# Two thirds of a gate product done as seven half products per unit

## The chip, the cores and the metric

The kernel runs on one core of a Trainium2 chip. TensorE (PE) does the matrix products, VectorE (DVE), ScalarE (ACT) and GpSimd (POOL) the element-wise work, and SyncE (SP) issues most DMAs. The time is the device time of one execution in microseconds, and a kernel is judged by the median of its runs. The kernel before takes 2010.5 us (three runs, 2009.51 to 2011.86).

## The reference

One layer for 1024 prompt frames and 32 sample frames, 1056 tokens of width 1024 in all. After attention, the recurrence and their mixing, the layer ends so:

```python
x = x + rms_norm(mix @ w_out, g_post_mix)
a, u = split(rms_norm(x, g_pre_ffn) @ w_up)             # 1024 -> 2 * 2816
ffn = (gelu(causal_conv3(a)) * u) @ w_down              # 2816 -> 1024
x = x + rms_norm(ffn, g_post_ffn)                       # called x2 below
y = x + (pe @ w_ple) * sigmoid(x @ w_ple_gate)          # 1024 -> 1024, the gate
```

All of it is float32. The change concerns `x @ w_ple_gate` and what it is added into.

## The kernel before

**Precision.** Every large product is made of three. Each operand is split into a high part, rounded to the type that PE multiplies in, and a low part, the rest; then high times high, high times low and low times high are summed in PSUM. `product` (L195 to L202) does that: for each of the k tiles of 128 rows three matmuls, L200, L201 and L202. A split costs ACT a copy (the high part) and DVE a subtraction (the low part): `split` at L223/L224 for activations, `load_next` at L181/L184 for weights.

**Layout and tiling.** Activations are held with the features on the 128 partitions and the tokens along the free axis. From w_down on, the tokens are worked in three thirds of 352 (`G3`, counted g = 0, 1, 2).

**w_up.** The stage before w_down multiplies by Winograd's form of Strassen's scheme: a 2 by 2 block product is done with seven half products instead of eight. The loop is `up_unit`. For every unit DVE and ACT make seven weight operands (`unit_parts`, L1444/L1445), POOL makes their four sums of 128x512 (L1451, L1452, L1453, L1458), and DVE joins the seven results out of PSUM (L1678 to L1694). The operands come out of a ring of eight buffers (tag `wb`).

**w_down.** `for g in range(3)`: for each half q of the output columns, 11 slabs of weights pass by, each used for four banks of PSUM. `d_out` copies the results to `acc` and sums their squares. When a third is through, `x2_start` and `x2_rows` make the norm's row factors, and `x2_part` makes one tile of 128x352 of x2 each time it is called: a scaled multiply (L1818), an addition of x1 (L1819), which a DMA brings in, and the split into `xh`, `xl` (L223, L224). For the first two thirds this is spread over the next third's w_down; for the last third it is spread over the gate stage.

**The gate stage.** Four weight tiles at a time are held (`ws`), and for each the thirds pass by: 24 blocks of 24 matmuls, each one bank of PSUM. `y_out` takes a block out: a tanh on ACT (L1861), then two DVE instructions (L1862 and L1863), the second with a factor 0.5 that makes a sigmoid of the tanh; `pl`, the product `pe @ w_ple`, is read back from memory by a DMA. `y_done`, one block later, turns the tile with three PE transposes (L1875), copies it on ACT (L1888, L1889), and every second tile goes to memory.

**Order.** The program order in the file is the priority; a scheduler fixes each engine's order when the kernel is built, and on the chip each engine goes through its own list in that order, waiting on semaphores. So an instruction that waits holds up everything behind it on its engine. SP's list of DMAs is one such list. A tile pool gives buffers by tag, and a new tile of a tag waits until an earlier one is released; tag `t` has six buffers, which the squares, the x1 tiles and the y tiles share.

Of the kernel before, what the change touches and what calls it, by code (L numbers as in the profile page):

```python
# [10 lines left out]
F32 = mybir.dt.float32  # L11
# [6 lines left out]
P = 128  # L18
D = 1024
KT = 8  # L20
# [39 lines left out]
def layer_kernel(  # L60
# [17 lines left out]
    def nm(s):  # L78
        n_names[0] += 1
        return f"{s}_{n_names[0]}"  # L80
# [56 lines left out]
    def rows_cols(src, r0, c, n, kt):  # L137
        return src[0, r0:r0 + kt * P, c:c + n].rearrange("(k p) c -> p k c", p=P), kt, n
# [81 lines left out]
    def split(hi, lo, src, scale=None):  # L220

        if scale is None:
            S.copy(hi, src)  # L223
            V.tensor_tensor(lo, src, hi.bitcast(F32), op=ALU.subtract)  # L224
# [10 lines left out]
    def mm_bank():  # L235
        return bank(pp, "mm", 3)
# [936 lines left out]
    with right("mp") as mp:  # L1173
# [238 lines left out]
    def ple_product(g, beside):  # L1412
        xs = pT.pop(g)
        for c in range(8):
            if c % 4 == 0:
                t = oz.tile([P, 4, H], F32, tag="x4", name=nm("ple"), bufs=3)
            b = block(ple_w[c // 4], slice((c % 4) * P, (c % 4 + 1) * P),
                      [xs[:, 0, k, :] for k in range(2)], [xs[:, 1, k, :] for k in range(2)],
                      ((0, 0), (1, 1)), H)
            S.copy(t[:, c % 4, :], b[:, :H])  # L1420
# [43 lines left out]
    def part_tile(i=0):  # L1464
        return wp.tile([P, 2, 4, P], F32R, tag="wb", name=nm("wt"), bufs=8)
# [266 lines left out]
    for u in range(NF):  # L1732
        if u == 1:
            Up = page(lq, 2, [P, 2, T], "Up")
        if u == NF - 1:
            limit[0] = len(plan)
            load_raw()
            load_raw()
        up_unit(u)
# [4 lines left out]
    def page_at(s, shape, name):  # L1744
        return page(lq if s[0] == "l" else rp, s[1:], shape, name)
# [31 lines left out]
    xh, xl = [None] * 3, [None] * 3  # L1777

    def d_out(g, c, b):
        S.copy(acc[g][c].bitcast(F32), b[:, :M3])  # L1780
# [8 lines left out]
    def x2_start(g):  # L1789
        rss[g] = norm_sums(ep, sqd[g], T96, 1.0 / D)  # L1790

    todo = []
    x2_r = {}

    def x2_rows(g):
        rb = ep.tile([P, M3], F32, tag="rb", name=nm("rb"), bufs=2)
        norm_rows(rss[g], T96, rb[:])
        if g == 0:
            x2_r[0] = page_at("l5", [P, 6, M3], "x2r")
            xh[0], xl[0] = third("r4", x2_r[0], 0, "xh"), third("l2", x2_r[0], 1, "xl")  # L1800
        elif g == 1:
            x2_r[1] = page_at("l3", [P, 6, M3], "x2r")
            xh[1] = third(chunk_at[0][0], x2_r[1], 0, "xh")
            xl[1] = third(chunk_at[0][1], x2_r[1], 1, "xl")
        else:
            xh[2] = third(chunk_at[1][0], x2_r[0], 2, "xh")
            xl[2] = third(chunk_at[1][1], x2_r[1], 2, "xl")
        todo.extend((g, k, rb) for k in range(KT))

    def x2_part(count=1, upto=-1):  # L1810

        while todo and (count > 0 or todo[0][0] <= upto):
            count -= 1
            g, k, rb = todo.pop(0)
            x1 = ep.tile([P, M3], F32, tag="t", name=nm("x1"), bufs=6)
            dma(x1[:], x1_d[:, k, M3 * g:M3 * g + M3])
            ak = acc[g][k].bitcast(F32)
            V.scalar_tensor_tensor(ak, ak, g_pffn[:, k:k + 1], rb[:], op0=ALU.mult, op1=ALU.mult)  # L1818
            V.tensor_tensor(ak, ak, x1[:], op=ALU.add)  # L1819
# [26 lines left out]
    for s, dst in ((0, o_pconv), (1, o_sconv)):  # L1846
        b = tr_bank()
# [3 lines left out]
        dma(dst[0, 0].rearrange("j (f p) -> (j f) p", p=P), t[:])  # L1851


    def y_out(g, c, b):
        y = ep.tile([P, M3], F32, tag="t", name=nm("y"), bufs=6)
        pl = ep.tile([P, M3], F32, tag="pl", name=nm("pl"), bufs=3)
        dma(pl[:], ple_d[:, c, M3 * g:M3 * g + M3])
        a = acc[g][c].bitcast(F32)
        cols = [slice(0, M3)] if (g, c) != (2, 7) else [slice(c_, c_ + m_) for c_, m_ in T96]
        for z_ in cols:  # L1860
            S.activation(y[:, z_], b[:, z_], AF.Tanh, scale=0.5)  # L1861
            V.scalar_tensor_tensor(y[:, z_], y[:, z_], 1.0, pl[:, z_], op0=ALU.add, op1=ALU.mult)  # L1862
            V.scalar_tensor_tensor(y[:, z_], y[:, z_], 0.5, a[:, z_], op0=ALU.mult, op1=ALU.add)  # L1863
        return y

    late, yrs = [], {}

    def y_done(g, c, y):

        if c % 2 == 0:  # L1870
            yrs[g] = ep.tile([P, 3, 256], F32, tag="yr", name=nm("yr"), bufs=4)
        yr = yrs[g]
        t = tr_bank()
        for i, (c_, m_) in enumerate(T96):
            E.transpose(t[:m_, i * P:(i + 1) * P], y[:, c_:c_ + m_], ident[:])  # L1875
        col = (c % 2) * P
        o = M3 * g
        fc = slice((c - 1) * P, (c + 1) * P)
# [9 lines left out]
        S.copy(yr[:, 0:2, col:col + P], t[:, :2 * P].rearrange("p (a b) -> p a b", b=P))  # L1888
        S.copy(yr[:96, 2, col:col + P], t[:96, 2 * P:3 * P])  # L1889
        if c % 2:  # L1890
            dma(y_prompt[0, o:o + 2 * P, fc].rearrange("(a p) c -> p a c", p=P), yr[:, 0:2, :])
            dma(y_prompt[0, o + 2 * P:o + 2 * P + m_, fc], yr[:m_, 2, :])
            if m_ < 96:
                dma(y_sample[0, :, fc], yr[m_:96, 2, :])

    for q in range(2):
        ws = [next_w(0) for _ in range(4)]
        for g in range(3):
            x2_part(0, g)
            for c in range(4):  # L1900
                if q == 0 and g == 0 and c == 1:
                    x2_start(2)
# [4 lines left out]
                late.append((g, 4 * q + c, y_out(g, 4 * q + c, b)))  # L1907
                if len(late) > 1:
                    y_done(*late.pop(0))
    for l in late:  # L1910
        y_done(*l)


# [30 lines left out]
```

## Time and profile before

| | |
|---|---|
| median of 3 runs | 2010.5 us |
| the profiled execution: time | 2014.52 us |
| the profiled execution: span, first to last instruction | 2012.8 us |
| granted TensorE clock, mean | 0.996 |
| PE busy in the span | 1985.5 us |
| DVE, ACT, POOL busy in the span | 1433.6, 965.6, 226.2 us |

The profile gives, for one execution, each engine's busy time, groups of instructions by line, single instructions in order of time, and waits. A group's row is: line, engine, operation, output from inputs, shape, count | busy us, mean ns of one | idle time before. A row of the instructions in order of time is: start in us, duration, engine, line, operation, names, count, and in brackets the idle time before it and what ended it. Matmuls overlap one another, so that the distance from one start to the next, and not the duration, tells how fast PE goes; the same holds, by less, for DVE and ACT.

### The profile page before, as it was taken

What the parts mean: (1) busy time and instruction counts of PE and PEld (TensorE: products, weight loads), DVE (VectorE), ACT (ScalarE), POOL (GpSimd) and SP (SyncE); (2) the same over time, 40 slices, a digit from 0 to 9 for tenths busy, and PEclk for the clock granted to TensorE, in tenths of its full rate; (3) what the DMA queues carried; (4) which work ended last, traced back from release to release, by engine and by line L of the source; (5) the groups of instructions that cost most, each with busy time, mean ns of one, the idle gap of its engine ahead of it and who ended that gap; (6) DMA issues with size and microseconds to landing.
All of it is one profiled execution on the core that took longest, in us unless ns stands there. A gap on an engine that the chain in (4) does not pass through costs nothing.

```text
span 2012.8 us, 37342 instructions
## 1 busy us (share of the span) xinstructions
PE 1985.5 (99%) x14282; PEld 1955.1 (97%) x14282; DVE 1433.6 (71%) x3193; ACT 965.6 (48%) x2184; POOL 226.2 (11%) x318
## 2 busy tenths in 40 slices
PE   7999999999999999999999999999999999999998
PEld 6999999999999999999999999999999999999998
DVE  5788888688888888554455778788887884655552
ACT  5655566556666666542124763333333344444432
POOL 2010100000000000002001123332333310000000
PEclk8999999999999999999999999999999999999999
DMA  8322321411111111377558582222222246655542
GB/s 263 96 94 68 115 64 53 144 54 57 37 54 37 54 53 56 118 229 230 165 167 291 164 296 64 85 75 85 68 92 65 88 137 202 214 190 172 167 129 82
DMA packets 250807, 245.31 MB, mean 122 GB/s; under 512 B 13365, under 2 KB 218696, under 8 KB 250629
## 3 DMA queue, kind: packets, MB, share of 16 engines
q1 hardware_dynamic: 242085, 214.92, 34.2%
q0 software_dynamic: 8464, 27.94, 3.9%
q8 instruction: 112, 1.84, 0.4%
q14 instruction: 66, 0.54, 0.1%
q10 hardware_dynamic: 80, 0.07, 0.0%
HBM read 177.56 MB, written 65.32 MB: 121 GB/s over the span
## 4 chain that ended last, share of the span: by engine, by line
PE 85%; DVE 5%; issue 2%; DMA 1%; ACT 1%; POOL 1%; SPq 0%; POOLq 0%; ACTq 0%; DVEq 0%
PE mm L200 13%; PE mm L201 13%; PE mm L202 13%; PE st L1667 7%; PE st L1665 7%; PE st L1666 7%; PE G L839 2%; PE Y L836 2%; PE G L838 2%; PE G L836 2%; PE Y L839 2%; PE Y L838 2%; PE tr L469 1%; PE X L836 1%; PE so L1030 1%
## 5 line engine op out<-in xcount | busy, mean ns | idle before, releaser
L1665 PE MATMUL st<-op,wt 128*128 128x264 f32 x1232 | 349.1, 284 | 3.7 <-ACT ple L1420 2.3
L1667 PE MATMUL st<-op,wt 128*128 128x264 f32 x1232 | 350.2, 284 | 0.0
L1666 PE MATMUL st<-op,wt 128*128 128x264 f32 x1232 | 348.4, 283 | 0.0
L184 DVE TENSOR_TENSOR wl<-wr,wh 128x1024 fp32r<-128x1024 f32 x132 | 161.6, 1225 | 129.3 <-ACT wh L181 115.5
L1665 PEld LDWEIGHTS st<-op,wt 128*128 128x128 f32 x1232 | 231.8, 188 | 4.8 <-ACT ple L1420 2.5
L1666 PEld LDWEIGHTS st<-op,wt 128*128 128x128 f32 x1232 | 232.1, 188 | 0.0
L1667 PEld LDWEIGHTS st<-op,wt 128*128 128x128 f32 x1232 | 231.5, 188 | 0.0
L181 ACT CAST wh<-wr 128x1024 fp32r<-128x1024 f32 x116 | 121.8, 1050 | 200.8 <-PE mm L201 146.5
L200 PE MATMUL mm<-ac,wh 128*128 128x352 f32 x528 | 170.7, 323 | 0.9 <-DVE Sp L1694 0.9
L201 PE MATMUL mm<-ac,wh 128*128 128x352 f32 x528 | 169.1, 320 | 0.0
L202 PE MATMUL mm<-ac,wl 128*128 128x352 f32 x528 | 169.1, 320 | 0.0
L1444 ACT CAST wt<-wu 128x512 fp32r<-128x512 f32 x126 | 77.7, 619 | 188.4 <-POOL ab L1651 93.7
L200 PE MATMUL mm<-La,wh 128*128 128x384 f32 (+1 forms) x504 | 166.2, 330 | 0.3 <-ACT kt L340 0.3
L201 PE MATMUL mm<-Lb,wh 128*128 128x384 f32 (+1 forms) x504 | 162.2, 322 | 0.0
L202 PE MATMUL mm<-La,wl 128*128 128x384 f32 (+1 forms) x504 | 162.2, 322 | 0.0
L200 PE MATMUL mm<-Ra,wh 128*128 128x264 f32 x512 | 145.5, 284 | 0.0
L201 PE MATMUL mm<-Rb,wh 128*128 128x264 f32 x512 | 145.0, 283 | 0.0
L202 PE MATMUL mm<-Ra,wl 128*128 128x264 f32 x512 | 145.0, 283 | 0.0
L1445 DVE TENSOR_TENSOR wt<-wu,wt 128x512 fp32r<-128x512 f32 x126 | 101.2, 806 | 39.7 <-ACT wt L1444 39.7
L453 ACT ACTIVATE sc<-sc,st 128x257 f32<-128x257 f32 (+1 forms) x144 | 69.6, 485 | 74.8 <-DVE st L448 73.6
L200 PEld LDWEIGHTS mm<-ac,wh 128*128 128x128 f32 x528 | 99.0, 188 | 1.2 <-DVE Sp L1694 1.2
L201 PEld LDWEIGHTS mm<-ac,wh 128*128 128x128 f32 x528 | 99.2, 188 | 0.0
(478 smaller groups left out, 5732.6 us busy)
## 6 DMA issues: line engine op xcount, KB each, us to landing
wr<-in_w_down_dram SPq DMA_DIRECT2D x66, 512.0 KB
wu<-in_w_up_dram SPq DMA_DIRECT2D x42, 512.0 KB
wu<-in_w_in_dram SPq DMA_DIRECT2D x32, 512.0 KB
wr<-in_w_in_dram SPq DMA_DIRECT2D x26, 512.0 KB
ac<-act_d SPq DMA_DIRECT2D x66, 176.0 KB
act_d<-Up SPq DMA_DIRECT2D x21, 528.0 KB
wr<-in_w_out_dram SPq DMA_DIRECT2D x16, 512.0 KB
pw_d<-pw POOLq DMA_DIRECT2D x11, 512.0 KB, 5.1
```

The costliest lines, as they stand in the source:

```text
L181: S.copy(hi[:], raw[:])
L184: V.tensor_tensor(lo[:], raw[:], hi[:].bitcast(F32), op=ALU.subtract)
L200: E.matmul(ps, wh, a, start=first and n == 0, stop=False)
L201: E.matmul(ps, wh, b, start=False, stop=False)
L202: E.matmul(ps, wl, a, start=False, stop=last and n == len(ks) - 1)
L836: E.matmul(o, wh, x[0][k], start=first and k == 0, stop=False, skip_group_check=True)
L838: E.matmul(o, wh, x[1][k], start=False, stop=False, skip_group_check=True)
L839: E.matmul(o, wl, x[0][k], start=False, stop=k == 3, skip_group_check=True)
L1445: V.tensor_tensor(t[:, 1], src, t[:, 0].bitcast(F32), op=ALU.subtract)
L1665: E.matmul(o, wh, xh, start=first and k == 0, stop=False, skip_group_check=True)
L1666: E.matmul(o, wh, xl, start=False, stop=False, skip_group_check=True)
L1667: E.matmul(o, wl, xh, start=False, stop=k == 3, skip_group_check=True)
```

## The change

The gate product of the first two thirds (704 tokens) is done as in w_up, by seven half products. The weight is cut into four units of 256 output columns; each unit is a 2 by 2 block of 512 by 128, and the two thirds of x2, each cut in two halves of 512 features, are the other 2 by 2 block. A half product is 12 matmuls (four k tiles of three) of 352 columns. The last third keeps blocks of 24.

- The activation operands for the seven products (`gate_ops`, 14 steps) are made while the last third of w_down runs (`op_steps`). For this x2 of the second third is made earlier, two tiles at a time in the first half of that third, and x2 of the first two thirds is no longer split itself.
- The weights of the units come as quarters of 128 rows by 4 by 128, 16 in all through five buffers (`quarter_load`), and `gate_parts` makes the seven operands of each unit from them, three products ahead in program order (`gate_prepare(n + 3)`). The four sums of a unit are made by DVE for the first unit and by POOL for the other three. For the last third the same weight is loaded again in eight tiles.
- `gate_unit` joins the seven results: one ACT copy and five DVE instructions per unit, from PSUM. Three of a unit's four outputs then go through `y_out` in place, their last addition on POOL; the fourth, and the last third's outputs, are added on DVE.
- `x2_start(2)`, `x2_rows(2)` and the eight `x2_part` calls of the last third stand after the half products n = 1, 3 and 5 to 12.
- `y_done` is called two half products later, not one block later. The buffers for its output go from four to three.
- The factor 0.5 moves to the exit of `pe @ w_ple` far earlier (`S.mul` for `S.copy`, L1420), so that the last step of `y_out` is a plain addition.

The diff, cut to its core:

```diff
-            S.copy(t[:, c % 4, :], b[:, :H])
+            S.mul(t[:, c % 4, :], b[:, :H], 0.5)
...
-            split(xh[g][k], xl[g][k], ak)
+            if g == 2:
+                split(last_x(0, k), last_x(1, k), ak)
...
+    def gate_parts():
+        def parts(src):
+            t = part_tile()
+            S.copy(t[:, 0], src)
+            V.tensor_tensor(t[:, 1], src, t[:, 0].bitcast(F32), op=ALU.subtract)
+            gate_w.append(t)
+        for u in range(4):
+            n = 4 * u
+            a11, a21, a22, a12 = (quarters[(n + i) % 5] for i in range(4))
+            s1 = wp.tile([P, 4, P], F32, tag="wb", name=nm("sa"), bufs=8)[:]
+            adder = V if u == 0 else G
+            parts(a11)
+            adder.tensor_tensor(s1, a21, a22, op=ALU.add)
+            adder.tensor_tensor(a21, a11, a21, op=ALU.add)
+            adder.tensor_tensor(a11, a11, s1, op=ALU.add)
+            yield
+            parts(a11)
+            yield
+            parts(a12)
+            adder.tensor_tensor(a12, a12, a11, op=ALU.add)
+            quarter_load(n + 5)
+            yield
...
-                if g == 1 and (q or k > 8) or g == 2 and q:
+                if g == 1 and (q or k > 8):
                     x2_part()
+                if g == 2 and q == 0 and 8 < k < 18:
+                    x2_part(2)
+                if g == 2:
+                    op_steps({18: 1, 20: 1}.get(k, 0) if q == 0 else
+                             {0: 1, 2: 2, 4: 1, 6: 1, 8: 1, 12: 1, 14: 2, 16: 1, 18: 1, 20: 1}.get(k, 0))
+                    if q and k == 18:
+                        gate_first()
+                    if q and k == 20:
+                        gate_prepare(3)
...
-            V.scalar_tensor_tensor(y[:, z_], y[:, z_], 0.5, a[:, z_], op0=ALU.mult, op1=ALU.add)
+            adder.tensor_tensor(y[:, z_], y[:, z_], a[:, z_], op=ALU.add)
...
+    def gate_unit(u):
+        X, Y, Z = (mm_bank() for _ in range(3))
+        x, y, zz = (t[:, :M3] for t in (X, Y, Z))
+        s1c, U2, nU3 = (um[:, i] for i in range(3))
+        c = 2 * u
+        for i, (t, first) in enumerate(((x, True), (y, True), (x, False), (y, False), (zz, True),
+                                        (y, False), (zz, False))):
+            n = 7 * u + i
+            gate_prepare(n + 3)
+            if n == 25:
+                limit[0] = len(plan)
+                load_next()
+            w = gate_w[n]
+            for k in range(4):
+                h, r = k // 2, k % 2
+                a, b = gate_rows(i, 0, h)[:, r, :], gate_rows(i, 1, h)[:, r, :]
+                E.matmul(t, w[:, 0, k, :], a, start=first and k == 0, stop=False,
+                         skip_group_check=True)
+                E.matmul(t, w[:, 0, k, :], b, start=False, stop=False, skip_group_check=True)
+                E.matmul(t, w[:, 1, k, :], a, start=False, stop=k == 3, skip_group_check=True)
+            if n == 1:
+                x2_start(2)
+            if n == 3:
+                x2_rows(2)
+            if n > 4:
+                x2_part()
...
+            if i == 0:
+                S.copy(s1c, x)
+            elif i == 1:
+                V.tensor_tensor(U2, s1c, y, op=ALU.subtract)
+            elif i == 2:
+                late.append((n, 0, c, y_out(0, c, x, r)))
+            elif i == 3:
+                V.tensor_tensor(nU3, y, s1c, op=ALU.subtract)
+            elif i == 4:
+                V.tensor_tensor(r, nU3, zz, op=ALU.subtract)
+                late.append((n, 1, c + 1, y_out(1, c + 1, r, r)))
+            elif i == 5:
+                V.tensor_tensor(r, y, s1c, op=ALU.subtract)
+                late.append((n, 0, c + 1, y_out(0, c + 1, r, r)))
+            else:
+                V.tensor_tensor(r, U2, zz, op=ALU.add)
+                late.append((n, 1, c, y_out(1, c, r, r)))
+            while late and late[0][0] + 2 <= n:
+                y_done(*late.pop(0)[1:])
...
-    for q in range(2):
-        ws = [next_w(0) for _ in range(4)]
-        for g in range(3):
-            x2_part(0, g)
-            for c in range(4):
-                if q == 0 and g == 0 and c == 1:
-                    x2_start(2)
-                if q == 0 and g == 0 and c == 3:
-                    x2_rows(2)
-                b = block(ws[c], ALL, xh[g], xl[g], KS, M3)
+    for u in range(4):
+        gate_unit(u)
+    xh, xl = ([last_x(part, k) for k in range(KT)] for part in range(2))
+    for c in range(8):
+        w = next_w(2)
+        b = block(w, ALL, xh, xl, KS, M3)
+        late.append((0, 2, c, y_out(2, c, b)))
+        while len(late) > 1:
+            y_done(*late.pop(0)[1:])
```

More of the change, by code (lines that the diff above doesn't have):

```diff
@@ L1735, in layer_kernel @@
         if u == NF - 1:
-            limit[0] = len(plan)
+            limit[0] = len(plan) - 8
             load_raw()
@@ L1776, in layer_kernel, with slots, gate_rows @@
     sqd = [None] * 3
-    xh, xl = [None] * 3, [None] * 3
+    slot_pages, slot_tiles = ("l5", "l3", "r4", "l2", "l4", "r3", "l6", "r5", "l7", "r6", "r0", "r7"), {}
+    def slots(n, m):
+        p = n // 6
+        if p not in slot_tiles:
+            slot_tiles[p] = page_at(slot_pages[p], [P, 6, M3], "gx")
+        return slot_tiles[p][:, n - 6 * p:n - 6 * p + m, :]
+    gate_at = {4: 0, 1: 8, 5: 16, 0: 24, 2: 32, 3: 40, 6: 48}
+    def gate_rows(j, part, h):
+        return slots(gate_at[j] + 4 * part + 2 * h, 2)
     def d_out(g, c, b):
@@ L1792, in layer_kernel @@
     todo = []
-    x2_r = {}
     def x2_rows(g):
@@ L1797, in x2_rows @@
         norm_rows(rss[g], T96, rb[:])
[L1798 to L1807, printed above, removed]
         todo.extend((g, k, rb) for k in range(KT))
@@ L1819, in x2_part, with last_x, gate_ops, rows @@
             V.tensor_tensor(ak, ak, x1[:], op=ALU.add)
-            split(xh[g][k], xl[g][k], ak)
+            if g == 2:
+                split(last_x(0, k), last_x(1, k), ak)
+    def last_x(part, k):
+        return slots(56 + 8 * part + k, 1)[:, 0, :]
+    um = ep.tile([P, 3, M3], F32, name="um")
+    def gate_ops():
+        def rows(g, k):
+            return acc[g][k], acc[g][k + 1]
+        def parts(j, h, src):
+            hi, lo = gate_rows(j, 0, h), gate_rows(j, 1, h)
+            if isinstance(src, tuple):
+                for i in range(2):
+                    split(hi[:, i, :], lo[:, i, :], src[i].bitcast(F32))
+            else:
+                split(hi, lo, src)
+        def sums(a, b, op):
+            for i in range(2):
+                p, q = (x[i].bitcast(F32) if isinstance(x, tuple) else x[:, i, :] for x in (a, b))
+                V.tensor_tensor(t[:, i, :], p, q, op=op)
+        t = um[:, 0:2, :]
+        b11, b21 = ([rows(0, o + 2 * h) for h in range(2)] for o in (0, 4))
+        b12, b22 = ([rows(1, o + 2 * h) for h in range(2)] for o in (0, 4))
+        for h in range(2):
+            sums(b11[h], b12[h], ALU.subtract)
+            parts(4, h, t)
+            yield
+            sums(b22[h], t, ALU.add)
+            parts(1, h, t)
+            yield
+            sums(b21[h], t, ALU.subtract)
+            parts(5, h, t)
+            yield
+        for j, b in ((0, b11), (2, b21)):
+            for h in range(2):
+                parts(j, h, b[h])
+                yield
+        for h in range(2):
+            sums(b12[h], b22[h], ALU.subtract)
+            parts(3, h, t)
+            yield
+        for h in range(2):
+            parts(6, h, b22[h])
+            yield
@@ new lines, in layer_kernel, with quarter_load, gate_first @@
+    quarters, gate_w = [], []
+    def quarter_load(n):
+        if n >= 16:
+            return
+        u, j = divmod(n, 4)
+        c, k0 = ((2 * u, 0), (2 * u + 1, 0), (2 * u + 1, 4), (2 * u, 4))[j]
+        dma(quarters[n % 5], rows_cols(w_ple_gate, k0 * P, c * P, P, 4)[0])
+    def gate_first():
+        for _ in range(2):
+            t = wp.tile([P, 2, 4, P], F32, tag="wr", name=nm("wr"), bufs=2)
+            quarters.extend(t[:, i] for i in range(2))
+        quarters.append(ep.tile([P, 4, P], F32, name="wr5")[:])
+        for n in range(5):
+            quarter_load(n)
@@ new lines, in gate_parts @@
+    def gate_parts():
[13 more added lines that the diff above has]
+            adder.tensor_tensor(a11, a11, s1, op=ALU.add)
+            yield
+            parts(a11)
+            yield
+            parts(a12)
+            adder.tensor_tensor(a12, a12, a11, op=ALU.add)
+            quarter_load(n + 5)
+            yield
+            parts(a21)
+            quarter_load(n + 6)
+            yield
+            parts(s1)
+            yield
+            parts(a22)
+            quarter_load(n + 7)
+            yield
+            parts(a12)
+            quarter_load(n + 8)
+            yield
@@ L1822, in layer_kernel, with gate_prepare, op_steps @@
+    gate_gen, op_gen = gate_parts(), gate_ops()
+    def gate_prepare(n):
+        while len(gate_w) < min(n + 1, 28):
+            next(gate_gen)
+    def op_steps(n):
+        for _ in range(n):
+            next(op_gen)
     for g in range(3):
@@ L1851, in layer_kernel, with y_out @@
         dma(dst[0, 0].rearrange("j (f p) -> (j f) p", p=P), t[:])
-    def y_out(g, c, b):
-        y = ep.tile([P, M3], F32, tag="t", name=nm("y"), bufs=6)
+    def y_out(g, c, b, y=None):
+        adder = V if y is None else G
+        if y is None:
+            y = ep.tile([P, M3], F32, tag="t", name=nm("y"), bufs=6)
         pl = ep.tile([P, M3], F32, tag="pl", name=nm("pl"), bufs=3)
@@ L1868, in y_done @@
     def y_done(g, c, y):
-        if c % 2 == 0:
-            yrs[g] = ep.tile([P, 3, 256], F32, tag="yr", name=nm("yr"), bufs=4)
-        yr = yrs[g]
+        second = (g, c // 2) in yrs
+        if not second:
+            yrs[g, c // 2] = ep.tile([P, 3, 256], F32, tag="yr", name=nm("yr"), bufs=3)
+        yr = yrs[g, c // 2]
         t = tr_bank()
@@ L1877, in y_done @@
         o = M3 * g
-        fc = slice((c - 1) * P, (c + 1) * P)
+        fc = slice((c // 2) * 256, (c // 2 + 1) * 256)
         m_ = min(96, 1024 - o - 2 * P)
@@ L1889, in y_done @@
         S.copy(yr[:96, 2, col:col + P], t[:96, 2 * P:3 * P])
-        if c % 2:
+        if second:
             dma(y_prompt[0, o:o + 2 * P, fc].rearrange("(a p) c -> p a c", p=P), yr[:, 0:2, :])
@@ L1894, in y_done @@
                 dma(y_sample[0, :, fc], yr[m_:96, 2, :])
-    for q in range(2):
-        ws = [next_w(0) for _ in range(4)]
-        for g in range(3):
-            x2_part(0, g)
-            for c in range(4):
-                if q == 0 and g == 0 and c == 1:
-                    x2_start(2)
-                if q == 0 and g == 0 and c == 3:
-                    x2_rows(2)
-                b = block(ws[c], ALL, xh[g], xl[g], KS, M3)
-                x2_part()
-                late.append((g, 4 * q + c, y_out(g, 4 * q + c, b)))
-                if len(late) > 1:
-                    y_done(*late.pop(0))
+    def gate_unit(u):
[23 more added lines that the diff above has]
+            if n > 4:
+                x2_part()
+            r = None
+            if i in (2, 4, 5, 6):
+                r = ep.tile([P, M3], F32, tag="t", name=nm("y"), bufs=6)[:]
+            if i == 0:
[12 more added lines that the diff above has]
+                late.append((n, 0, c + 1, y_out(0, c + 1, r, r)))
+            else:
+                V.tensor_tensor(r, U2, zz, op=ALU.add)
+                late.append((n, 1, c, y_out(1, c, r, r)))
+            while late and late[0][0] + 2 <= n:
+                y_done(*late.pop(0)[1:])
@@ L1910, in layer_kernel @@
+    for u in range(4):
[7 more added lines that the diff above has]
+            y_done(*late.pop(0)[1:])
     for l in late:
-        y_done(*l)
+        y_done(*l[1:])
 _INS = ['x_prompt', 'x_sample', 'cache_win_k', 'cache_win_v', 'state_hgrn', 'cache_ffn_conv',
```

## The prediction

> **What bounds the kernel now.** I read the page first: busy shares, then the chain that ended last.
>
> ```profile
> span 2012.8 us, 37342 instructions
> PE 1985.5 (99%) x14282; PEld 1955.1 (97%) x14282; DVE 1433.6 (71%) x3193; ACT 965.6 (48%) x2184; POOL 226.2 (11%) x318
> ...
> PE 85%; DVE 5%; issue 2%; DMA 1%; ACT 1%; POOL 1%; SPq 0%; POOLq 0%; ACTq 0%; DVEq 0%
> ```
>
> PE bounds the whole, so fewer matmuls can pay. What they pay is decided in the stage that changes, so next the busy times by stretch: a piece of w_down, its last third, and the gate stage.
>
> ```profile
> 1660.00:1740.00 80.00, 80.00 (x506) 80.00 (x505) 41.18 (x45) 36.41 (x49) 0.00 (x0) 1.00 0.64 212
> 1906.00:2006.00 100.00, 99.86 (x649) 99.16 (x648) 43.55 (x89) 29.41 (x85) 0.00 (x0) 1.00 0.39 111
> ...
> 1827.54:1909.34 81.80, 81.80 (x522) 81.73 (x520) 43.03 (x66) 32.08 (x48) 0.00 (x0) 1.00 0.48 158
> ```
>
> Columns: stretch, its length, busy PE, PE loading, DVE, ACT, POOL with counts, clock, DMA share, GB/s. PE has no gap in the gate stage, DVE and ACT are less than half busy, POOL does nothing. In w_down a matmul of 352 columns takes 80.00/506 = 0.158 us of PE. The gate stage has 576 of them (91.0 us); its other small PE instructions, 72 transposes and 12 for the norm, share the rest of the 100 us, about 0.125 us each, so the three transposes of an output tile cost 0.375.
>
> **What the change removes.** Two thirds: 16 blocks x 24 = 384 matmuls become 28 x 12 = 336. 48 x 0.158 = 7.6 us of PE, 0.38%; it cannot gain more, since nothing else is taken from PE. The same transposes stay.
>
> **What it adds, step by step.** A half product takes PE 12 x 0.158 = 1.9 us. Beside each, DVE now must do more than beside a block of 3.8 us. Its prices are the distances between starts, in the list of DVE's instructions in the gate stage (first row: the norm's first small operation, second: its last):
>
> ```profile
> 1909.89 0.22 DVE L1260 TENSOR_SCALAR nv<-tr 128x2 f32<-128x2 f32 x2 [2.01 <-PE tr L1257]
> ...
> 1912.78 0.16 DVE L217 SCALAR_TENSOR_TENSOR nr<-rst,nr 128x3 f32<-128x3 f32 x1
> ...
> 1919.07 0.53 DVE L1863 SCALAR_TENSOR_TENSOR y<-y,acc 128x352 f32<-128x352 f32 x1
> 1919.52 1.07 DVE L1818 SCALAR_TENSOR_TENSOR acc<-acc,gvec,rb 128x352 f32<-128x352 f32 x2
> 1920.51 0.52 DVE L1819 TENSOR_TENSOR acc<-acc,x 128x352 f32<-128x352 f32 x1
> 1920.94 1.08 DVE L1818 SCALAR_TENSOR_TENSOR acc<-acc,gvec,rb 128x352 f32<-128x352 f32 x2
> 1921.93 0.53 DVE L224 TENSOR_TENSOR xl<-acc,xh 128x352 fp32r<-128x352 f32 x1
> 1922.37 1.08 DVE L1818 SCALAR_TENSOR_TENSOR acc<-acc,gvec,rb 128x352 f32<-128x352 f32 x2
> ```
>
> An output's step (either of y_out's two on DVE) costs 0.45 us; a tile of x2 costs 0.495 (half of 0.99) + 0.43 + 0.44 = 1.37; the norm holds DVE for 3.0 (1909.89 to 1912.94). For the weight operands, the joins and POOL's sums the w_up stage has the rows; DVE first, then POOL in the same stretch:
>
> ```profile
> 1307.47 1.65 DVE L1622 SCALAR_TENSOR_TENSOR a<-ab,cvec,a 128x1058 f32<-128x1058 f32 x1 [1.34 <-ACT a L1621]
> 1309.15 2.23 DVE L1623 SCALAR_TENSOR_TENSOR a<-ab,cvec,a 128x1058 f32<-128x1058 f32 x1
> ...
> 1316.07 0.68 DVE L1445 TENSOR_TENSOR wt<-wu,wt 128x512 fp32r<-128x512 f32 x1
> 1316.66 0.70 DVE L1683 TENSOR_TENSOR Sp<-st,Sp 128x528 f32<-128x528 f32 x1
> 1317.28 1.46 DVE L1445 TENSOR_TENSOR wt<-wu,wt 128x512 fp32r<-128x512 f32 x1
> ```
>
> ```profile
> 1306.70 1.29 POOL L1451 TENSOR_TENSOR sa<-wu 128x512 f32<-128x512 f32 x1 [8.86 <-PE st L1667]
> 1308.07 2.19 POOL L1452 TENSOR_TENSOR wu<-wu,wu 128x512 f32<-128x512 f32 x1
> 1310.34 2.19 POOL L1453 TENSOR_TENSOR wu<-wu,sa 128x512 f32<-128x512 f32 x1
> ...
> 1316.89 1.30 POOL L1458 TENSOR_TENSOR wu<-wu 128x512 f32<-128x512 f32 x1 [4.33 <-DVE wt L1445]
> ```
>
> ```profile
> L1678 DVE TENSOR_TENSOR Sp<-Sp,st 128x528 f32<-128x528 f32 x21 | 14.5, 692 | 0.0
> ...
> L1685 DVE TENSOR_TENSOR us<-Sp,st 128x264 f32<-128x264 f32 x1 | 0.4, 423 | 0.0
> ```
>
> ```profile
> L1623 DVE SCALAR_TENSOR_TENSOR a<-ab,cvec,a 128x1058 f32<-128x1058 f32 x1 | 1.3, 1317 | 0.0
> ```
>
> A weight operand costs DVE 0.6 us (1316.07 to 1316.66). A join of 352 columns lies between 0.423 (264) and 0.692 (528): 0.51 long, some 0.08 of it overlapped as in the rows above, 0.43. POOL's sum of 512 takes 1.29 alone, so one of 352 some 0.89. And the two engines hold each other up: L1445, 0.68 alone, took 1.46 beside L1458, 0.77 lost (L1683, which reads PSUM, lost nothing); L1623, 1.32 in the last unit, where POOL does nothing, took 2.23 beside L1452, 0.91 lost; L1622 lost 0.33. POOL's own sums went from 1.29 to 2.19. I charge DVE 0.77 for each sum of 512, the row of the very instruction that the change uses, and 0.53 (0.77 x 352/512) for each of 352.
>
> On that the Trainium skill, "SBUF — State Buffer", section "Who interferes with whom", is stricter: a DVE instruction with two SBUF inputs and a GpSimd one that reads SBUF exclude each other, and the loser blocks for the whole instruction. The trace agrees: L1452 ended at 1310.26, 1.11 us after L1623 began, and 1.11 + 1.32 is 2.43 against 2.23 measured. What the rule would give here is the third rival below.
>
> **The sum.** The heavy stretch is products 2 to 13: the norm, all eight x2 tiles, and POOL's sums for units 1 and 2.
> - PE: 144 matmuls x 0.158 = 22.75, six outputs' transposes 2.25, the norm's twelve small ones 1.5: 26.5 us.
> - DVE: norm 3.0; 12 operands x 0.6 = 7.2; 9 joins x 0.43 = 3.9; 10 output steps x 0.45 = 4.5; 8 x2 tiles x 1.37 = 10.9: 29.5 us.
> - POOL's hold on DVE: 8 sums of 512 x 0.77 = 6.2, 6 of 352 x 0.53 = 3.2: 9.4 us. (Nothing at the low end; all its time, 8 x 1.29 + 6 x 0.89 = 15.6, at the high end.)
>
> DVE needs 38.9 us where PE needs 26.5: 12.4 too many. Two things soften it. In products 0 and 1 DVE has 3.8 - 2.1 = 1.7 us free to make operands ahead. And each join has one product's time before PE needs its bank: 1.9 - 0.43 = 1.5. Once DVE is later than that, PE stops at the join, because joins stand in the same list behind x2 tiles and operands. PE stalls 12.4 - 1.7 - 1.5 = 9.2 us (low end 29.5 - 26.5 - 3.2, nothing; high end 15.4).
> - Products 14 to 27: DVE fits (7 operands, 5 joins, 5 output steps per unit, 8.6 of 14.8 us, and POOL's 4.7), except the burst 18 to 20, where four sums and three outputs meet: 9.1 against 6.5, less 1.5: 1.1 us (0 to 3).
> - POOL orders its three sums for the next unit ahead of an output's addition; at 2.19 each an output can be 6 us late, where its transposes come two products, 3.8 us, later and all matmuls stand behind them. Up to 2.8 us in each of three units; I take 1.0 in all (0 to 8), as sums start as soon as a buffer comes free (what ended L1451's idle time was PE).
> - Start: product 0 needs the first operand, whose quarter is asked for at k = 18, two slabs (7.6 us) before w_down ends. A DMA of activations took 4.64 (row below), the split 0.6 + 0.6, and DVE then makes three sums at 0.6: 7.6 us for the second operand, due 1.9 after the end. I take 1.0 (0 to 3) for waiting behind the last squares.
>
> ```profile
> 1635.47 4.64 DMA ac<-act_d
> ```
>
> Hidden, at nothing: the 14 operand steps in w_down's last third add some 17 us to DVE's 43.0 of 81.8, and ACT's to its 32.1; without that room they would cost PE 17. ACT in a unit: seven copies, one join, four tanh, four exits, 9.2 us of 14.8, from these rows:
>
> ```profile
> L1861 ACT ACTIVATE y<-mm 128x352 f32<-128x352 f32 x23 | 10.7, 464 | 51.8 <-PE mm L202 51.8
> ...
> L1888 ACT COPY yr<-tr 128x256 f32<-128x256 f32 x23 | 8.5, 370 | 0.4 <-PE tr L1875 0.3
> ...
> L1889 ACT COPY yr<-tr 96x128 f32<-96x128 f32 x23 | 6.2, 271 | 0.0
> ```
>
> ```profile
> L1444 ACT CAST wt<-wu 128x512 fp32r<-128x512 f32 x122 | 75.3, 618 | 185.4 <-POOL ab L1651 93.7 <-PE st L1667 67.7 <-DVE wt L1445 23.9
> ```
>
> The 0.5 at L1420: a copy of 264 columns takes 389 ns, one scaled by a vector (L1279) 487; at worst 0.1 us on ACT under six matmuls, and nothing (at most 0.3) on PE. The weight is read twice, 4 MB more in 90 us where 111 GB/s flow: nothing. SP issues 16 quarter loads among those of `pl` and x1; the one behind POOL's fourth sum waits for it and holds the next `pl`, a loss inside the 0 to 8 above.
>
> ```profile
> L1420 ACT COPY ple<-mm 128x264 f32<-128x264 f32 x32 | 11.8, 389 | 6.4 <-PE mm L202 5.3 <-DMA ple_d<-ple 1.0
> ...
> L1279 ACT ACTIVATE z<-mm,gph 128x264 f32<-128x264 f32 x9 | 4.4, 487 | 4.4 <-PE mm L202 4.4
> ```
>
> Total: -7.6 + 9.2 + 1.1 + 1.0 + 1.0 = +4.7 us. On the profiled execution, span 2012.8 and time 2014.52, that is 2017.5 and 2019.2. That execution stands 4.0 above the median of the runs; on the median, 2010.5 + 4.7 = 2015.2. The ends of all terms: -7.6 and -7.6 + 15.4 + 3 + 8 + 3 = +21.8.
>
> **The rivals.**
> A, faster: POOL hardly delays DVE, because its sums fall where DVE waits or reads PSUM, as L1683 beside L1458. Then the heavy stretch costs nothing (29.5 - 26.5 is under 3.2) and with the three small terms at half, 1.6, the time is 2010.5 - 6.0 = 2004.5. For it: L1622 lost only 0.33. Against it: DVE has no idle time there. It decides where the 14 sums cost DVE less than 0.2 us each.
> B, no change: x2's later steps slide. In the profile before, additions of x1 came one per block (they wait for tag `t`), and only the first multiplies ran ahead. If the additions and splits, 0.87 x 8 = 7.0 us, reach products 14 to 27, where DVE has room, the stall is 2.2 and not 9.2: 2008.2. Against it: their place in the order is 5 to 12, and a waiting addition blocks DVE.
> C, much slower: the full exclusion. POOL's 15.6 us all fall on DVE, the stall is 15.4, the others as I took them: 2010.5 - 7.6 + 15.4 + 3.1 = 2021.4, and up to 2027 if an output's addition also stops PE twice.
>
> **How the numbers follow.** My forecast (its own range 2011 to 2019) has 0.36, A 0.27, B 0.19, C 0.18. The last row of chances counts from 0.2%, 4.0 us, about what a measurement of this kernel can tell: A is faster; B is within, and 0.06 of the forecast's lower part; the rest of it and C slower: 0.27, 0.25, 0.48. The range leaves out half of A's gain below 2004 and C above 2023.
>
> **What would show it.** In the profile after: 48 matmuls fewer at 0.158; DVE near 9 tenths busy in the first two units, PE gaps there put down to DVE's joins (U2, nU3, r); L1445's counterpart and the x2 steps above 0.7 beside POOL's sums; units 0 and 1 some 4 and 5 us longer than 14.8, units 2 and 3 near it. Wrong, if the units run at 14.8 each or if the waits are on ACT, quarters or transposes.

## The result, and the profile after

The changed kernel takes 2018.9 us (median of 6 runs, 2017.64 to 2019.92), the kernel before 2011.75 beside it. The ratio is 1.0036, 95% interval 1.0023 to 1.0049: slower by about 7 us, where 4.7 were forecast.

The page of the kernel after, first lines:

```profile
span 2016.6 us, 37464 instructions
PE 1979.0 (98%) x14234; PEld 1946.8 (97%) x14234; DVE 1479.0 (73%) x3249; ACT 985.5 (49%) x2220; POOL 261.8 (13%) x346
```

PE's instructions fell by 48, as the diff says, but its busy time only by 6.5 us, and the span grew. The spans of two single executions cannot be set against each other to a few us: the first matmul of w_down starts at 1649.44 in the profile before and at 1644.51 after, though one scale factor and a limit on weights loaded ahead are all that differs before it, and among the profiles below it moved between 1643 and 1651. So I compare the last stage alone, from the turning of the conv tails behind the last product of w_down (L1848 before, L1976 after) to the end. Busy times of that stretch, before and after (length, PE, PE loading, DVE, ACT, POOL, clock, DMA share, GB/s):

```profile
1905.10:2012.80 107.70, 102.47 (x664) 101.13 (x661) 45.40 (x96) 31.91 (x94) 0.00 (x0) 1.00 0.38 109
```

```profile
1901.23:2016.60 115.37, 99.98 (x616) 95.92 (x613) 76.57 (x126) 48.99 (x123) 35.93 (x28) 0.97 0.48 141
```

The stage, called "the stage" from here on, went from 107.7 to 115.4 us: 7.7 more, about what the medians show (7.1); w_down itself took 255.7 and 256.7. PE idles 15.4 us in it, where it idled 5.2. And it is busy 99.98 us for work that a later kernel with the same PE instructions does in 96.40: the mean granted clock is 0.97, at half for two stretches of 3.41 us (shown in the last section). The 0.98 of that later kernel (all on DVE, below) lies behind PE's last product. What PE waited for, after, from w_down on (engine and line waited for, us, times, longest):

```profile
PE tr L2007 <- POOL y L1994: 5.4, 5, 2.3
PE tr L301 <- DVE nr L217: 3.9, 1, 3.9
PE mm L200 <- ACT sq L1802: 0.9, 1, 0.9
PE tr L2007 <- DVE y L1994: 0.9, 1, 0.9
PE mm L2045 <- DVE y L2067: 0.4, 1, 0.4
PE mm L2045 <- DVE um L2061: 0.2, 1, 0.2
```

The wait for L1802 lies in w_down, the rest in the stage; the 0.9 us for DVE's L1994 belongs to the last output, and the kernel before has it too. The joins (L2061, L2067) hardly stall PE. It stands at the norm's rows of the last third (L301) and at the transposes of outputs whose last addition is POOL's (L1994). The list of DVE's instructions around the first of these waits:

```profile
1906.02 0.22 DVE L1260 TENSOR_SCALAR nv<-tr 128x2 f32<-128x2 f32 x2
1908.84 0.69 DVE L1899 TENSOR_TENSOR wt<-wr,wt 128x512 fp32r<-128x512 f32 x1 [2.59 <-ACT wt L1898]
1909.45 0.16 DVE L211 TENSOR_SCALAR rsb<-nv 128x3 int32<-128x3 int32 x1
...
1910.63 0.16 DVE L216 TENSOR_TENSOR rst<-rst,nv 128x3 f32<-128x3 f32 x1
...
1911.82 0.88 DVE L215 SCALAR_TENSOR_TENSOR rst<-nr 128x3 f32<-128x3 f32 x1
1912.74 1.18 DVE L216 TENSOR_TENSOR rst<-rst,nv 128x3 f32<-128x3 f32 x1
1913.96 0.16 DVE L217 SCALAR_TENSOR_TENSOR nr<-rst,nr 128x3 f32<-128x3 f32 x1
```

```profile
1908.18 0.62 ACT L1898 CAST wt<-wr 128x512 fp32r<-128x512 f32 x1 [4.14 <-POOL wr L1910]
```

```profile
1906.87 1.28 POOL L1910 TENSOR_TENSOR wr<-wr,sa 128x512 f32<-128x512 f32 x1
1911.31 1.38 POOL L1994 TENSOR_TENSOR y<-y,acc 128x352 f32<-128x352 f32 x1 [3.16 <-DVE nr L217]
1912.65 1.26 POOL L1915 TENSOR_TENSOR wr<-wr,wr 128x512 f32<-128x512 f32 x1
```

Two things are to be seen. The norm's third small operation stands behind an operand (L1899 at 1908.84), which stands behind ACT's copy, which stands behind POOL's sum L1910: a wait in DVE's list. And operations on three elements, 0.16 us long, take 0.88 and 1.18 when POOL's addition and sum run beside them.

Units 0 to 3 took 21.0, 21.5, 17.1 and 15.6 us (from the first matmul of each to that of the next), where PE needs about 14.8.

### The profile page after: what moved, and what is told of

Its sections match the earlier page's. It is cut to its first block, busy times and chain, and to the rows that moved or that the text cites. A ratio compares the mean times of both kernels' runs of the same rounds, so it can differ in the third digit from the quotient of the medians.

```text
span 2016.6 us, 37464 instructions
## 1 busy us (share of the span) xinstructions
PE 1979.0 (98%) x14234; PEld 1946.8 (97%) x14234; DVE 1479.0 (73%) x3249; ACT 985.5 (49%) x2220; POOL 261.8 (13%) x346
```

## The experiments

The theories are those of the expectations: 1, POOL's work holds up DVE's instructions (hold); 2, the chain from POOL's sums through the operands (chain); 3, the burst of x2 tiles and the norm. Where POOL's work is given to DVE, the expectations call something else theory 2: that VectorE has too much work of its own. Where the edit leaves something out, the expectation says so. The times before stood between 2010.9 and 2011.5 beside each group of runs.

**POOL's sums left out.**

```diff
-            adder.tensor_tensor(s1, a21, a22, op=ALU.add)
-            adder.tensor_tensor(a21, a11, a21, op=ALU.add)
-            adder.tensor_tensor(a11, a11, s1, op=ALU.add)
+            if u == 0:
+                adder.tensor_tensor(s1, a21, a22, op=ALU.add)
+                adder.tensor_tensor(a21, a11, a21, op=ALU.add)
+                adder.tensor_tensor(a11, a11, s1, op=ALU.add)
+            else:
+                s1 = a22
...
-            adder.tensor_tensor(a12, a12, a11, op=ALU.add)
+            if u == 0:
+                adder.tensor_tensor(a12, a12, a11, op=ALU.add)
```

> The twelve sums that GpSimd makes for the weight operands of units 1 to 3 are left out (the raw quarters stand in for them, so the gate of the first two thirds is computed with the wrong operands). Theory 1, hold: GpSimd's sums block VectorE's two-input instructions; 12 x 0.77 = 9.2 us of VectorE time come back, most of it in units 0 and 1: 6 to 9 us less than the changed kernel, 2010 to 2013. Theory 2, chain: the operands wait for GpSimd's sums and VectorE's list stands behind them: the same gain, 6 to 9. Theory 3, burst: the eight x2 tiles and the norm are what VectorE is late with: 2 us less at most, 2017.

Measured: 2010.0 us, ratio to the kernel before 0.9990 (0.9978 to 1.0003), the stage 104.0, units 0 to 2 at 16.4, 17.0, 15.7:

```profile
1899.28:2003.30 104.02, 96.39 (x616) 93.22 (x613) 68.86 (x126) 49.07 (x123) 17.17 (x16) 0.99 0.54 157
```

The twelve sums are worth 11.4 us of the stage (8.9 by the medians; the profiled execution was the fastest of its ten). The x2 tiles, the norm and all of DVE's own work are still there, at their places, so the burst alone costs little; theory 3 falls. DVE's busy time fell by 7.7 us (76.57 to 68.86), 0.64 for each sum.

**Sums that are made but not used.** The sums go into a buffer of the operands' ring, and the operands are made of the raw quarters.

```diff
+                sp = a22
+                adder.tensor_tensor(s1, a21, a22, op=ALU.add)
+                adder.tensor_tensor(s1, a11, a21, op=ALU.add)
+                adder.tensor_tensor(s1, a11, a22, op=ALU.add)
...
-            parts(s1)
+            parts(sp)
```

> The twelve sums are still made by GpSimd, of the same size, but into a buffer that nobody reads, and the operands are taken from the raw quarters (wrong operands again). Theory 1, hold: the time stays with the changed kernel, within 2 us of 2018.9. Theory 2, chain: it goes with the kernel without sums, 2010 to 2013. Theory 3: no change from the changed kernel.

Measured: 2019.7 us (1.0048, 1.0030 to 1.0066), the stage 116.7: as slow as the changed kernel. But it does not settle the matter, since an operand's buffer in the ring could still wait for POOL. So the same with a buffer of its own (`sink` in place of `s1`), which nothing waits for; what still follows on a sum is only the reloading of the quarter that it read:

> GpSimd's twelve sums go to a buffer of their own that is in no ring and that nothing ever reads or waits for (in the kernel with idle sums it came from the ring of the weight operands, so that an operand's buffer still waited for GpSimd). To make room, two tags whose second buffer is not needed have one. The operands are made from the raw quarters, so the gate of the first two thirds is wrong. Theory 1, hold: the mere presence of the sums costs; stage from the end of w_down 110 to 117, 2014 to 2020. Theory 2, chain: only waiting for them costs; stage 104 to 106, 2009 to 2012, as without the sums.

Measured: 2018.3 us (1.0034, 1.0023 to 1.0044), the stage 114.5:

```profile
1902.01:2016.50 114.49, 99.92 (x616) 96.20 (x613) 80.20 (x126) 49.29 (x123) 35.53 (x28) 0.97 0.49 142
...
L1900 DVE TENSOR_TENSOR wt<-wr,wt 128x512 fp32r<-128x512 f32 x23 | 24.5, 1074 | 0.7 <-ACT wt L1899 0.6
```

Of the 11.4 us, 10.5 come back (8.2 by the medians) though no instruction uses the sums, and operands, 0.68 us long without POOL, take 1.07 on the mean. DVE is busy 80.2 us and not 68.9, with the same instructions. The hold is shown, and it is enough without the chain. How much the chain adds in the changed kernel stays open: there DVE stood idle 4.8 us before operands that waited for ACT's copies (row further below), here 0.7, but the hold is heavier here, 11.3 us of DVE's time for the twelve sums against 7.7, so what is missing from the 11.4 does not bound the chain. "SBUF — State Buffer" of the Trainium skill, section "Who interferes with whom", has the rule: two SBUF inputs on DVE and a reading GpSimd instruction exclude each other, for a whole instruction. By that rule even three elements wait out a sum, and L216's 1.18 us above agrees.

**The x2 tiles later**, and **the norm later too**.

```diff
-            if n > 4:
+            if n > 13:
                 x2_part()
```

> Only the place of the last third's eight x2 tiles is changed: after products 14 to 21, not 5 to 12. Theory 3, burst, and theory 1 with it: 8 x 1.37 = 11 us leave the heavy stretch for products in which VectorE has room: unit 1 falls from 21.5 us to 16 or 17, units 2 and 3 gain 1 or 2: 4 to 6 us less, 2013 to 2015. Theory 2, chain: no change, within 1.5 us. The wait for the norm in unit 0 (3.9 us) stays by each.

Measured: 2022.6 us (1.0051, 1.0032 to 1.0071), the stage 114.3, units 22.1, 16.0, 20.2. Unit 1 fell as expected, but unit 2 took over what unit 1 lost, and the time did not fall. The 4 to 6 us of theories 3 and 1 did not come; the stage, 1.1 us shorter, stayed within theory 2's 1.5, while the median of these four runs lies 3.7 above the changed kernel's.

```diff
-            if n == 1:
+            if n == 8:
                 x2_start(2)
-            if n == 3:
+            if n == 11:
                 x2_rows(2)
```

> As the kernel with late x2 tiles, and the norm of the last third is moved too: its sums after product 8 and its rows after product 11, not 1 and 3. If the norm stalled TensorE in unit 0 because VectorE's small operations stand in a crowded place behind an operand that waits for a sum (theory 2 in that place), the 3.9 us and the slow clock behind them go: 4 to 6 us less than with late tiles alone, 2008 to 2010, below the kernel before. If GpSimd's hold is what slows it (theory 1), the wait shows again at its new place, and the gain is under 2 us.

Measured: 2017.8 us (1.0034, 1.0020 to 1.0049), the stage 112.4, units 14.5, 17.9, 22.5. The wait for the norm did go (3.9 to 0.7 us), so it was the crowded place that made it, and the sums in it: without them it was 0.8 us at the old place. But PE then waited 5.0 us for POOL's additions and 3.8 at joins. I read both kernels so that the hold moved with the load; no run shows that by itself. Nor do the numbers decide: against late tiles alone the median fell by 4.8 us, within the 4 to 6 of theory 2, but the stage by only 1.9, within the 2 of theory 1, and 2008 to 2010 was not reached.

**POOL's work given to DVE**: the sums (first line of the diff), the outputs' additions (second), and both. The additions are 16 and not 12 as I had counted: all four outputs of a unit go through `y_out` in place, so POOL adds all four (28 POOL instructions in the stage after: 12 sums and 16 additions).

```diff
-            adder = V if u == 0 else G
+            adder = V
...
-        adder = V if y is None else G
+        adder = V
```

> VectorE makes the sums of all four units (12 x 0.6 = 7.2 us more for it), GpSimd keeps the outputs' additions. If the cost of GpSimd's sums is their hold on VectorE's instructions (theory 1: leaving them out took 11.4 us off the stage from the end of w_down, 115.4 to 104.0), paying 7.2 of VectorE's own time for them is cheaper: the stage takes 109 to 112, the kernel 2012 to 2016. Theory 2, what costs is that VectorE has too much work of its own, whoever makes the sums: the stage stays at 114 to 117, 2018 to 2021.

Measured: 2014.3 us (1.0018, 1.0008 to 1.0027), the stage 111.3. As theory 1 has it.

> VectorE makes all outputs' additions (12 x 0.45 = 5.4 us more for it), GpSimd keeps the sums. TensorE's transposes then no longer wait for GpSimd (5.4 us in the changed kernel). Theory 1, hold: the additions cost VectorE 0.53 each by hold, so nothing is lost there, and the late transposes go: stage 111 to 114, 2014 to 2017. Theory 2, VectorE's own load: the wait only moves from the transposes to the joins, stage 115 to 118, 2018 to 2022.

Measured: 2019.1 us (1.0041, 1.0026 to 1.0057), the stage 116.2. Theory 2's numbers (VectorE's own load) were met and theory 1's were not: the late transposes now wait for DVE (4.7 us), the norm's wait stays (3.1), and joins stall 4.0. While POOL's sums run, 16 x 0.45 = 7.2 us more on DVE cost what the lighter hold saves; that is my reading, and the next run is its test.

> GpSimd does nothing in the stage: sums and additions are all VectorE's (12.6 us more for it). Theory 1, hold: stage 105 to 109, 2008 to 2013, as fast as the kernel before. Theory 2, VectorE's own load: 118 to 122, above 2020.

Measured: 2011.2 us (0.9994, 0.9982 to 1.0006), the stage 106.1, units 15.6, 16.0, 15.4. As fast as the kernel before, and 9.3 us of the stage better than the changed kernel, though DVE does 28 instructions more. The operand and output groups of the kernel after, and of this one, show what they pay:

```profile
L1899 DVE TENSOR_TENSOR wt<-wr,wt 128x512 fp32r<-128x512 f32 x19 | 17.0, 904 | 4.8 <-ACT wt L1898 4.8
...
L1993 DVE SCALAR_TENSOR_TENSOR y<-y,pl 128x352 f32<-128x352 f32 x14 | 10.5, 753 | 1.0 <-ACT y L1992 0.9
```

```profile
L1899 DVE TENSOR_TENSOR wt<-wr,wt 128x512 fp32r<-128x512 f32 x20 | 13.5, 684 | 0.6 <-ACT wt L1898 0.5
...
L1993 DVE SCALAR_TENSOR_TENSOR y<-y,pl 128x352 f32<-128x352 f32 x18 | 9.3, 519 | 1.5 <-ACT y L1992 1.4
```

```profile
1902.11:2008.20 106.09, 96.40 (x615) 93.02 (x613) 75.85 (x154) 49.03 (x123) 0.00 (x0) 0.98 0.53 154
```

DVE is busy for 75.85 us here and for 76.57 in the changed kernel: what POOL did was paid in full by DVE's waiting. "VectorE has too much work of its own" falls with this run. It takes the chain away together with the hold (the idle time before operands goes from 4.8 to 0.6), so by itself it does not part the two.

**The transposes later.**

```diff
-            while late and late[0][0] + 2 <= n:
+            while late and late[0][0] + 4 <= n:
```

> Only the transposes of an output are put four half products behind it, not two. If they came too early for a chain that is merely long (latency), the 5.4 us of waits for GpSimd's additions and the slow clock behind the longest go: stage 108 to 110, 2011 to 2014. If VectorE and GpSimd together have too much to do (theory 1), the wait shows elsewhere, at the joins, and the gain is under 2 us.

Measured: 2021.4 us (1.0056, 1.0037 to 1.0076), the stage 116.7. The transposes no longer wait for POOL, and the joins wait 4.6 us instead. So the late transposes look like a symptom.

**A better version.** All on DVE, transposes four products later; then also the x2 tiles spread (`if n > 5 and n % 2 == 0`); or the norm after 8 and 11 and the x2 tiles after 13 to 20.

> With GpSimd idle in the stage (as the kernel with all on VectorE), the transposes come four half products behind their output, not two. By theory 1 nothing else stalls the units: they run at 15 us each (15.6, 16.0, 15.4 in the kernel with all on VectorE) and 1 us comes off, 2009 to 2011. The late transposes left in the last third (4.0 us) wait for weights by DMA and stay.

> As that, and the eight x2 tiles stand after every second product from 6 to 20. If VectorE's own burst still costs something once GpSimd's hold is gone (theory 3 as a remainder), unit 1 falls from 16.0 to 15 us: 1 us less, 2008 to 2010. If the burst costs nothing, no change within 1 us.

> GpSimd idle, transposes four products behind, the norm after products 8 and 11 and the x2 tiles after products 13 to 20. If the crowd at the start of the stage is what is left, units 0 and 1 run at 15 us and the time is 2006 to 2009, below the kernel before; if VectorE's total is what is left (61 us of work beside 60 us of TensorE's), the stall moves to units 2 and 3 and the time stays at 2009 to 2012.

Measured: 2009.0 us (0.9986, 0.9977 to 0.9995), 2008.9 (0.9981, 0.9972 to 0.9991) and 2006.8 (0.9978, 0.9966 to 0.9989); the stages 104.2, 104.6 and 104.6. All three are faster than both kernels, by some 2 to 5 us below the kernel before; among themselves they cannot be told apart, and their intervals overlap that of the kernel with all on DVE (0.9982 to 1.0006). So neither the spread of the x2 tiles nor the crowd at the start is shown to cost anything once POOL is idle. Nor did the units gain together: the four took 63.0, 61.8 and 63.0 us, against 62.2 with all on DVE. In the second kernel unit 1 fell to 14.8, as expected, and unit 2 rose to 16.3; in the third unit 0 fell to 13.9 and unit 3 rose to 17.5. What the stage gained lies behind them, in the last third (43.8 us with all on DVE, then 41.0, 42.7 and 41.5), where no gain was expected. The last one's stage:

```profile
1904.64:2009.20 104.56, 96.16 (x616) 93.51 (x613) 76.60 (x154) 49.60 (x123) 0.00 (x0) 0.99 0.54 156
```

With 7.6 us of matmuls fewer the stage could be 100.1; 4.5 us are left. In the kernel with all on DVE transposes of the last third waited 3.1 us while ACT waited for weight tiles that come through two buffers; that was read from its profile and not tried.

## Why the prediction was right, and where it was not

- **The result** lies in the range and on the forecast side: +7.1 us on the medians, where 4.7 were forecast, at the upper end of the forecast's own range. In part that is luck. Of the stage's 7.7 us, PE's busy time gives -2.5 (6.1 less work, 3.6 more by the slower clock) and its idle time +10.2: 3.9 at the norm's rows, 5.4 at outputs, 0.6 at joins, 0.3 elsewhere. Against the sum, 8.6 too much at joins stands beside 11.9 too little at the norm, the outputs and the clock.
- **The gain of 7.6 us** is near: 48 PE instructions fewer. With all on DVE the matmuls alone are busy 7.3 us less than before (98.31 to 90.98), and PE in all 6.1 (102.47 to 96.40); where the difference lies was not traced.
- **The mechanism**, POOL's hold on a loaded DVE, is right. The pair of sums left out and sums that nobody uses shows it without the chain; the pair of POOL's work and the same work on DVE shows what both are worth. Its price was near: 0.64 us a sum, where 0.77 was charged, and 0.46 an addition, where 0.53 was (DVE is busy for 68.86 us in the kernel without sums, and for 75.85 with all on DVE, of which 12 x 0.6 + 16 x 0.45 = 14.4 are the work taken over; 68.86 - 61.45 is 7.4 for 16 additions). The same working on the other kernels gives 0.67 a sum with the additions on DVE, 0.56 an addition with the sums on DVE, and 0.94 a sum where nobody uses them, so a price holds for one arrangement. That there are 16 additions and not 12 was misread in the description of the change and in the sum; in the heavy stretch two output steps of DVE (0.9) become two more holds (1.1), which hardly moves it.
- **"PE stalls at the join"** is the step that failed. Joins stalled PE 0.6 us, not 9.2. DVE's lateness reached PE through the norm's rows (3.9, a wait charged nowhere: I had costed the norm's time on DVE, not who waits behind it) and through the outputs' transposes (5.4, where "1.0 in all" was taken). These make 9.3 of the 10.8 us that PE waited in the stage, and waits on transposes stood among the prediction's own signs of being wrong. The sum of the units' excess, 6 and 7 us in units 0 and 1 where 4 and 5 were named, was nearer than its place; DVE, named 9 tenths busy there, was busy 14.8 of 21.0 us in unit 0 and all of the 21.5 in unit 1. When the transposes were moved back, the joins took over the wait, as the step had it.
- **The heavy stretch** was drawn too sharply. I had the x2 tiles make products 2 to 13 heavy and gave products 14 to 27 room; rival B rested on that. Moving the tiles there gave 1.1 us of the stage and no time: later units seem as full once POOL's hold is counted, and unit 2 took 2.3 us too long even in the changed kernel, where 1.1 was taken.
- **The start** cost nothing in the stage: product 0 began 0.14 us after the turning of the tails. 1.0 was taken. The operand steps in w_down's last third were rightly costed at nothing, but for the 0.9 us that PE waited for ACT's squares (L1802) between the second third and the last.
- **The missing term** is the clock: about 3.6 us (99.98 against 96.40 busy; by the two half-clock stretches below, with 6.45 us of PE work in them, 3.2) that no row of before could show, as its gate stage had no gap.
- **Rival C**, full exclusion, was right as a rule (three elements wait out a sum) and too dear as a sum: 0.64 us a sum where it charged 1.29, presumably as not all of POOL's time meets an instruction with two SBUF inputs. **Rival A** fell: it needed less than 0.2.

## What to carry to other kernels

Before giving GpSimd element-wise work beside a busy VectorE, charge VectorE for it: here 0.64 us per sum and 0.46 per addition, and up to half as much again in other arrangements, at least what VectorE needed to do the same work itself (0.6 and 0.45). Halving the product behind each prepared operand doubles the rate of that preparation; add up the helpers' time per stage before counting matmuls saved. When a wait is moved and shows up elsewhere at the same length, look for the shared resource behind both.

## What was not expected of the hardware

A gap of a few us in PE's work costs more than itself. PE's instructions after the wait for the norm, and those after the 2.3 us wait for POOL:

```profile
1914.17 1.59 PE L301 MATMUL tr<-ident,nr 128*128 128x128 f32 x6 [3.94 <-DVE nr L217]
1915.47 0.64 PE L2048 MATMUL mm<-gx,wt 128*128 128x352 f32 x1
1915.91 0.50 PE L2045 MATMUL mm<-gx,wt 128*128 128x352 f32 x1
1916.20 0.50 PE L2047 MATMUL mm<-gx,wt 128*128 128x352 f32 x1
...
1917.31 0.32 PE L2048 MATMUL mm<-gx,wt 128*128 128x352 f32 x1
1917.47 0.32 PE L2045 MATMUL mm<-gx,wt 128*128 128x352 f32 x1
```

```profile
1929.46 0.55 PE L2007 MATMUL tr<-ident,y 128*128 128x128 f32 x3 [2.34 <-POOL y L1994]
...
1930.66 0.33 PE L2048 MATMUL mm<-gx,wt 128*128 128x352 f32 x1
...
1931.36 0.49 PE L2048 MATMUL mm<-gx,wt 128*128 128x352 f32 x1
1931.65 0.49 PE L2045 MATMUL mm<-gx,wt 128*128 128x352 f32 x1
```

Each engine's busy time around these places, in slices of 3.41 us, the granted clock third from the end:

```profile
1910.39:1913.80 3.41, 0.00 (x0) 0.00 (x0) 3.31 (x8) 0.17 (x1) 2.49 (x2) 1.00 0.19 53
1913.80:1917.21 3.41, 3.04 (x12) 3.04 (x13) 2.24 (x6) 0.45 (x1) 0.10 (x1) 0.50 0.49 147
...
1927.45:1930.87 3.42, 1.41 (x10) 1.41 (x11) 3.42 (x6) 0.61 (x2) 1.50 (x2) 1.00 0.51 152
1930.87:1934.28 3.41, 3.41 (x13) 3.41 (x12) 3.41 (x7) 1.59 (x5) 1.11 (x1) 0.50 0.85 221
```

Matmuls that start 0.16 us apart at the full clock start 0.29 apart in the second and the fourth of these slices, where the clock is 0.50: at once after the wait of 3.94 us, and 1.4 us late after the one of 2.34. After a wait of 1.40 us the distance stayed 0.16. "TensorE: Matmul & The Clock Gate" of the Trainium skill, Part 1, says that the clock falls to half after an idle window of about 3.4 us. The first fall agrees: PE was idle for the whole slice before it. Before the second PE was idle for only 2.0 of 3.4 us, so here the measurement decides: a slice need not be idle throughout.

What counts is how a wait lies in the slices. The falls and rises above are 3.41 us or a multiple of it apart. In all the profiles of these runs 14 falls lie in the stage ahead of PE's last product, each behind a slice in which PE was idle for 1.86 us or more, while slices with up to 1.78 us idle were followed by none (behind the last product 1.61 was enough). With all on DVE a wait of 2.36 us, from 1986.94 to 1989.30, fell into two slices, and the clock stayed:

```profile
1984.23:1987.64 3.41, 2.71 (x17) 2.42 (x16) 0.71 (x1) 1.79 (x5) 0.00 (x0) 1.00 0.71 195
1987.64:1991.06 3.42, 1.76 (x12) 1.79 (x13) 2.44 (x5) 0.94 (x4) 0.00 (x0) 1.00 0.19 53
1991.06:1994.47 3.41, 3.41 (x24) 3.39 (x23) 0.27 (x1) 0.77 (x3) 0.00 (x0) 1.00 0.58 159
```
